# Gelu of the state-space output beside its split, and residual-gate pieces spread over the first attention's fill

## The chip, the cores and the metric

The kernel runs on one core of one Trainium2 chip, as one program of 17,119 instructions. The metric is the device time of one execution in microseconds (us); a run of the kernel is given by its median over several executions. The engines are TensorE (PE; its weight loads PEld), VectorE (DVE), ScalarE (ACT), GpSimd (POOL) and SyncE (SP), whose queue here issues most of the loads.

## The reference

Two transformer blocks follow each other on 512 tokens of width 1024, in float32. The change lies in the first block. Cut to what matters there:

```
mod = silu(c) @ w_ada + b_ada;  shift, scale, gate = split(mod, 3)
h = rms_norm(x, norm_g) * (1 + scale) + shift
ssm_u, ssm_z, q, k, v, attn_z, q_idx, k_idx, w_idx = split(h @ w_in)
y = complex diagonal state-space scan of ssm_u, by groups of 16 channels
z = gelu(y);  z = z * sigmoid(z @ w_glu + b_glu)
y_ssm  = z * silu(ssm_z)
y_attn = sparse_attention(q, k, v, index scores) * silu(attn_z)
x = x + gate * (concat([y_ssm, y_attn]) @ w_out)
```

So the gelu has one reader, the gated product with `w_glu` and the factor in front of it; and the third of `w_ada` that gives `gate` (the residual gate) is read only where the block's output is added to `x`.

## The kernel before

All large products are made of three float32r products: a weight or an activation is split into a rounded half ("hi", one copy on ACT, L145) and the rest ("lo", one subtraction on DVE, L146), and `mm3` (L153 to L155) multiplies hi by hi, lo by hi and hi by lo. `wchunk` loads a weight piece of 512 KB into a tile `wraw` (three buffers), splits it into `whi` and `wlo` (four buffers each), and the products run over it. Activations lie transposed; `hT` is the normalised input in its two halves.

The first block runs in stages. After the projections, index scores and the scan, the attention over eight heads runs as the main stream (`attend`), about 11 us a head. Each head needs transposes of its keys (L734) and, every second head, of its queries (L727); ACT and DVE take their halves out of PSUM (`ksth`, `kstl`, `qst`). Scores are products on PE (L341, L342) into one of two PSUM tiles `ps_s`; DVE adds the mask tile `bm` and takes the row minimum (L343), ACT makes the exponential (L345), DVE the reciprocal (L752), POOL and DVE the scaling (L350, L352); PE transposes the result (L369) into one of two PSUM tiles `ps_t`, ACT copies it out (L375), and PE multiplies by the values (L383). The mask tiles have one buffer each and POOL makes them (L744, L745), so those of the next head wait for L343 of this one.

Beside it runs the fill: `weave` draws as many products of the remaining projections as the main stream allows. Before the change the fill is, in order: what is left of the attention's gate columns (`ga`, two weight pieces), all eight pieces of the residual gate (`gate_sums`), the first half of the state-space gate columns (`gs`, two pieces), the split of the gelu's output `z` into `zT` (`z_split`), the second half of `gs` (two pieces), and the product with `w_glu` (two pieces). A piece of the residual gate is a load of 512 KB into a `wraw` buffer on SP (L897) and one multiply-and-sum of 128x1024 on DVE (L898); it has no product on PE. The gelu itself is the last step of `ssm_out` (L1330, four tiles of 128x512, `zg` from `zi`), which ends before the attention begins.

PE and SP execute in the order in which the program is written. ACT, DVE and POOL are ordered by a list scheduler at build time; on the chip each engine then executes its list strictly in order, so an instruction that waits holds up all behind it.

Of the kernel before, what the change touches and what calls it, by code (L numbers as in the profile page):

```python
# [11 lines left out]
AF = mybir.ActivationFunctionType  # L12
# [92 lines left out]
class Kern:  # L105
# [139 lines left out]
    def both(self, *streams):  # L245
        for g in streams:
            yield from g

    def hold(self, time):
        yield time  # L250
# [197 lines left out]
    def block1(self):  # L448
        nc, A, tc = self.nc, self.A, self.tc
# [14 lines left out]
        hT = [self.pages("hT" + x, 8, F32R) for x in "hl"]  # L464
# [126 lines left out]
        w_in = A["w_in"]  # L591
# [60 lines left out]
        def proj(n, dst):  # L652
            s8 = sm.tile([128, 4, 8], F32, name="s8", tag="s8", bufs=2)

            def ev(j, c, p):
                if c == 0:
                    dst.append(self.pg("qk"))
                nc.scalar.copy(dst[j][:, c:c + 256], p)
                sq = sm.tile([128, 256], F32, name="sq5", tag="q256", bufs=2)
                nc.scalar.activation(sq, p, AF.Square)  # L660
                nc.vector.tensor_reduce(s8[:, j, c // 64:c // 64 + 4], sq.rearrange("p (h d) -> p h d", d=64), axis=AX.X, op=OP.add)

            yield from self.gemm_tn(hT, 8, w_in, n, 512, ev)
            sums.append(s8)
# [11 lines left out]
        def ev_gs(j, p):  # L676

            gates[0].append(self.pg("gs"))
            nc.scalar.activation(gates[0][j], p, AF.Tanh, scale=0.5)
            STT(out=gates[0][j], in0=gates[0][j], scalar=1.0, in1=p, op0=OP.add, op1=OP.mult)  # L680

        def ev_ga(j, p):
# [4 lines left out]
        z = self.pages("zg", 4)  # L687
        fill = self.both(proj(1024, qf), proj(1536, kf), self.gemm_tn(hT, 8, w_in, 2048, 512, ev_v),
                         self.gemm_nt(hT, 8, self.cols(w_in, 2560, 512), ev_ga))
# [96 lines left out]
        zT = []  # L786

        def z_split():
            zT.extend(self.pages("zT" + x, 4, F32R) for x in "hl")
            for k in range(4):  # L790
                self.split(z[k], zT[0][k], zT[1][k])
                yield 0.0

        fill = self.both(fill, self.gate_sums(), self.gemm_nt(hT, 8, self.cols(w_in, 512, 256), ev_gs), z_split(),
                         self.gemm_nt(hT, 8, self.cols(w_in, 768, 256), lambda j, p: ev_gs(2 + j, p)),
                         self.gemm_nt(zT, 4, self.cols(A["w_glu"], 0, 512), ev_glu))
        self.weave(self.attend([head(h) for h in range(8)], more=1.4), fill)
        self.dump("y", y[0])
        attp.__exit__(None, None, None)
# [502 lines left out]
    def ssm_out(self, z):  # L1302


        nc = self.nc
        zi = self.pages("zi", 4)
        zd = self.dr.tile([4, 128, S], F32, name="zdram")
        for q in range(2):
            p = [self.ps((128, 512), "t") for _ in range(2)]
            for m in range(8):  # L1310
                a = q * 8 + m
                o = [v[:, m * 64:(m + 1) * 64] for v in p]
                for b in range(2):
                    nc.tensor.matmul(o[b], lhsT=self.TO[:, :, :, 2 * a + b], rhs=self.U(2 * a + b), start=True, stop=False)  # L1314
                for x in range(2):
                    for b in range(2):
                        s = slice(b * 64, b * 64 + 64)
                        nc.tensor.matmul(o[b], lhsT=self.F[x][a // 4][s, a % 4 * 128:(a % 4 + 1) * 128], rhs=self.St[x][s, a, 0:64],  # L1318
                                         start=False, stop=x == 1)
                yield 1.3  # L1320
            for b in range(2):
                O = self.pg("O")
                nc.scalar.copy(O, p[b])
                nc.scalar.dma_start(zd[2 * q + b], O)
        yield 2.0
        for n in range(4):
            nc.sync.dma_start(zi[n].rearrange("p (t k) -> p t k", t=8), zd[n].rearrange("(t c) (g k) -> (c g) t k", t=8, g=8))
        yield 0.0
        for n in range(4):
            nc.scalar.activation(z[n].rearrange("p (k t) -> p t k", t=8), zi[n].rearrange("p (t k) -> p t k", t=8), AF.Gelu_apprx_tanh)  # L1330
        self.dump("z", z)


    def block2(self):
# [525 lines left out]
```

## Time and profile before

| | us |
|---|---|
| median of 3 runs (1253.65 to 1254.65) | 1253.88 |
| the profiled execution | 1255.27 |
| its span, first to last instruction | 1253.5 |
| PE, DVE, ACT, POOL busy in it | 1159.3, 815.6, 552.8, 459.5 |
| attention of the first block, about | 254 to 372 |

The sum of a change is made against the profiled execution, whose own time is 1.39 us above the median. The chain that ended last runs for 76% of the span through PE and for 15% through DVE. In the timelines a row gives the start, the duration, the engine, the line, the tiles, the shape, and in brackets how long the engine had been idle before it and what released it. A busy PE can still be slow: the granted clock is given by stretch.

### The profile page before, as it was taken

To read this page: it belongs to the slowest core of one execution; us is meant where nothing else is said; L and a number is where in the kernel's file an instruction comes from. 1 tells how busy PE (TensorE), PEld (TensorE's weight loads), DVE (VectorE), ACT (ScalarE), POOL (GpSimd) and SP (SyncE) were. 2 spreads that over 40 slices of the span, in tenths; PEclk is the share of its full clock that TensorE was granted. 3 is DMA by queue.
4 is the path that set the end of the run, shared out by engine and by line. 5 is a ranking of instruction groups with operands and counts; after the bars stand their busy time and mean duration, and the time that the engine had idled before them with its cause. 6 is when DMAs were issued, how large, how long until landed. Compare 5 with 4: busy or idle time off the path is not lost.

```text
span 1253.5 us, 17119 instructions
## 1 busy us (share of the span) xinstructions
PE 1159.3 (92%) x6264; PEld 949.0 (76%) x6264; DVE 815.6 (65%) x1587; ACT 552.8 (44%) x1038; POOL 459.5 (37%) x546
## 2 busy tenths in 40 slices
PE   2786888977899999989999999999999999999998
PEld 2576887955678998977777777788888888888876
DVE  6887999267755466795667666554677743677731
ACT  4434432065744444555565656333544421344420
POOL 3869998068522135355656565201000000000000
PEclk9897989988999999998999999999999999999999
DMA  9452122163134532221111111134333223333330
GB/s 356 143 154 67 35 85 72 35 210 110 34 121 154 154 107 87 85 75 51 38 47 35 34 35 34 52 119 132 101 101 100 83 91 97 106 96 86 103 106 34
DMA packets 112755, 118.05 MB, mean 94 GB/s; under 512 B 16184, under 2 KB 101216, under 8 KB 112672
## 3 DMA queue, kind: packets, MB, share of 16 engines
q1 hardware_dynamic: 102432, 107.20, 27.1%
q10 hardware_dynamic: 10240, 9.77, 2.4%
q8 instruction: 49, 0.80, 0.3%
q14 instruction: 34, 0.28, 0.1%
HBM read 109.47 MB, written 6.30 MB: 92 GB/s over the span
## 4 chain that ended last, share of the span: by engine, by line
PE 76%; DVE 15%; ACT 3%; POOL 2%; issue 2%; DMA 1%; SPq 0%; ACTq 0%; DVEq 0%; POOLq 0%
PE ps_g L153 20%; PE ps_g L154 20%; PE ps_g L155 19%; PE ps_t L369 4%; PE ps_o L383 4%; DVE wlo L146 2%; PE ps_s L342 2%; PE ps_s L341 2%; DVE wada L490 1%; PE ps_t L1314 1%; DVE score L965 1%; DVE score L948 1%; PE ps_o L1652 1%; DVE t L1059 1%; PE ps_t L1318 1%
## 5 line engine op out<-in xcount | busy, mean ns | idle before, releaser
L145 ACT CAST whi<-wraw 128x1024 fp32r<-128x1024 f32 (+4 forms) x161 | 161.6, 1010 | 170.2 <-PE ps_g L154 146.7
L146 DVE TENSOR_TENSOR wlo<-wraw,whi 128x1024 fp32r<-128x1024 f32 (+4 forms) x143 | 175.8, 1235 | 61.3 <-ACT whi L145 60.8
L153 PE MATMUL ps_g<-hT,whi 128*128 128x512 f32 x504 | 205.1, 407 | 0.0
L155 PE MATMUL ps_g<-hT,wlo 128*128 128x512 f32 x504 | 198.9, 395 | 0.0
L154 PE MATMUL ps_g<-hT,whi 128*128 128x512 f32 x504 | 198.1, 393 | 0.0
L350 POOL TENSOR_TENSOR P<-P,rsum 128x256 f32<-128x256 f32 (+3 forms) x144 | 100.6, 728 | 77.9 <-DVE rsum L1439 29.7
L345 ACT ACTIVATE P<-P,nm 128x128 f32<-128x128 f32 (+3 forms) x160 | 89.6, 560 | 84.0 <-DVE nm L343 82.8
L153 PEld LDWEIGHTS ps_g<-hT,whi 128*128 128x128 f32 x504 | 95.2, 189 | 26.0 <-issue 9.3
L155 PEld LDWEIGHTS ps_g<-hT,wlo 128*128 128x128 f32 x504 | 95.0, 189 | 19.9
L154 PEld LDWEIGHTS ps_g<-hT,whi 128*128 128x128 f32 x504 | 95.3, 189 | 18.8 <-issue 1.2
L343 DVE CUSTOM_DVE_ANT_0 P<-ps_s,att 128x128 f32<-128x128 f32 (+3 forms) x128 | 62.1, 485 | 51.4 <-PE ps_t L369 26.9
L369 PE MATMUL ps_t<-consts,P 128*128 128x128 f32 x400 | 67.5, 284 | 12.2 <-DVE qst L889 7.1
L153 PE MATMUL ps_g<-whi,hTh 128*128 128x256 f32 x192 | 60.7, 316 | 13.8 <-DVE iq L886 8.0
L153 PE MATMUL ps_g<-act,whi 128*128 128x512 f32 (+1 forms) x176 | 70.2, 399 | 0.0
L154 PE MATMUL ps_g<-act,whi 128*128 128x512 f32 (+1 forms) x176 | 69.1, 393 | 0.0
L155 PE MATMUL ps_g<-act,wlo 128*128 128x512 f32 (+1 forms) x176 | 69.0, 392 | 0.0
L369 PEld LDWEIGHTS ps_t<-consts,P 128*128 128x128 f32 x400 | 47.6, 143 | 27.3 <-issue 14.9
L849 POOL TENSOR_TENSOR acc<-acc,sq 128x512 f32<-128x512 f32 x15 | 21.9, 1462 | 118.0 <-ACT sq L848 115.5
L154 PE MATMUL ps_g<-wlo,hT 128*128 128x256 f32 (+1 forms) x208 | 58.7, 282 | 2.4 <-DVE wlo L146 2.4
L153 PE MATMUL ps_g<-whi,hT 128*128 128x256 f32 (+1 forms) x208 | 59.0, 284 | 1.4 <-ACT sq L1354 1.4
L154 PE MATMUL ps_g<-wlo,hTh 128*128 128x256 f32 x192 | 56.3, 293 | 4.0 <-DVE wlo L146 4.0
L155 PE MATMUL ps_g<-whi,hT 128*128 128x256 f32 (+1 forms) x208 | 58.6, 282 | 0.0
(509 smaller groups left out, 2916.1 us busy)
## 6 DMA issues: line engine op xcount, KB each, us to landing
wraw<-in_w_in_dram SPq DMA_DIRECT2D x56, 512.0 KB, 3.6
wraw<-in_w_up_dram SPq DMA_DIRECT2D x40, 512.0 KB, 3.6
wada<-in_w_ada_dram SPq DMA_DIRECT2D x16, 512.0 KB, 7.4
wraw<-in_w_down_dram SPq DMA_DIRECT2D x16, 512.0 KB, 3.4
wadag<-in_w_ada_dram SPq DMA_DIRECT2D x8, 512.0 KB, 4.5
wraw<-in_w_out_dram SPq DMA_DIRECT2D x8, 512.0 KB, 3.4
wraw<-in_w_attn_br_dram SPq DMA_DIRECT2D x8, 512.0 KB, 3.4
wraw<-in_w_o_dram SPq DMA_DIRECT2D x8, 512.0 KB, 3.5
```

The lines of the kernel that those rows point to most:

```text
L145: nc.scalar.copy(hi, src)
L146: (eng or nc.vector).tensor_tensor(out=lo, in0=src, in1=hi, op=OP.subtract)
L153: mm(out, lhsT=l[0], rhs=r[0], start=start, stop=False)
L154: mm(out, lhsT=l[0], rhs=r[1], start=False, stop=False)
L155: mm(out, lhsT=l[1], rhs=r[0], start=False, stop=stop)
L341: nc.tensor.matmul(s, lhsT=q, rhs=khi[:, :w], start=True, stop=False)
L342: nc.tensor.matmul(s, lhsT=q, rhs=klo[:, :w], start=False, stop=True)
L343: nc.vector.tensor_tensor_reduce(out=P[i], in0=s, in1=madd(i), scale=-1.0, scalar=3.0e38, op0=OP.add, op1=OP.min, accum_out=nm[:, i:i + 1])
L345: nc.scalar.activation(P[i], P[i], AF.Exp, scale=-1.0, bias=nm[:, i:i + 1], accum_out=sums[:, i:i + 1])
L350: nc.gpsimd.tensor_tensor(out=P[n], in0=P[n], in1=sc[:, n:n + 1].to_broadcast([128, (n + 1) * 128]), op=OP.mult)
L369: nc.tensor.transpose(pt[:, o:o + 128], P[i][:, j * 128:(j + 1) * 128], self.ident)
L383: nc.tensor.matmul(acc[x * 64:(x + 1) * 64, j * 128:], lhsT=V(j), rhs=tiles[b][:, o:o + w], start=start and j == 0, stop=stop and j == 2)
```

## The change

The four gelu instructions leave the end of `ssm_out` and are issued in `z_split`, just ahead of the split of their output. `gate_sums` leaves its place in the fill's sequence; a new helper `between` runs the rest of the fill and issues one piece of the residual gate after every 4.0 us of estimated product time (a step of three 128x512 products counts as 0.648, so one piece after every seven steps). What is computed stays the same.

```diff
--- before.py
+++ after.py
@@ -245,6 +245,16 @@
     def both(self, *streams):
         for g in streams:
             yield from g
+
+    def between(self, main, other, every):
+
+        due = every
+        for got in main:
+            yield got
+            due -= got
+            if due <= 0 and next(other, None) is not None:
+                due = every
+        self.go(other)
 
     def hold(self, time):
         yield time
@@ -788,12 +798,14 @@
         def z_split():
             zT.extend(self.pages("zT" + x, 4, F32R) for x in "hl")
             for k in range(4):
+                nc.scalar.activation(z[k].rearrange("p (k t) -> p t k", t=8), self.zi[k].rearrange("p (t k) -> p t k", t=8), AF.Gelu_apprx_tanh)
+            for k in range(4):
                 self.split(z[k], zT[0][k], zT[1][k])
                 yield 0.0
 
-        fill = self.both(fill, self.gate_sums(), self.gemm_nt(hT, 8, self.cols(w_in, 512, 256), ev_gs), z_split(),
-                         self.gemm_nt(hT, 8, self.cols(w_in, 768, 256), lambda j, p: ev_gs(2 + j, p)),
-                         self.gemm_nt(zT, 4, self.cols(A["w_glu"], 0, 512), ev_glu))
+        fill = self.between(self.both(fill, self.gemm_nt(hT, 8, self.cols(w_in, 512, 256), ev_gs), z_split(),
+                                      self.gemm_nt(hT, 8, self.cols(w_in, 768, 256), lambda j, p: ev_gs(2 + j, p)),
+                                      self.gemm_nt(zT, 4, self.cols(A["w_glu"], 0, 512), ev_glu)), self.gate_sums(), 4.0)
         self.weave(self.attend([head(h) for h in range(8)], more=1.4), fill)
         self.dump("y", y[0])
         attp.__exit__(None, None, None)
@@ -1326,9 +1338,7 @@
         for n in range(4):
             nc.sync.dma_start(zi[n].rearrange("p (t k) -> p t k", t=8), zd[n].rearrange("(t c) (g k) -> (c g) t k", t=8, g=8))
         yield 0.0
-        for n in range(4):
-            nc.scalar.activation(z[n].rearrange("p (k t) -> p t k", t=8), zi[n].rearrange("p (t k) -> p t k", t=8), AF.Gelu_apprx_tanh)
-        self.dump("z", z)
+        self.zi = zi
 
 
     def block2(self):
```

On PE the order of the instructions does not change. On SP, from the last loads of the scan's output (`zi`) to the loads of `w_out`, there stood before:

```order
L1327 DMA zi<-zdram 128x8x64 x4
L174 DMA wraw<-in_w_in_dram 128x4x256 x2
L897 DMA wadag<-in_w_ada_dram 128x1024 x8
L174 DMA wraw<-in_w_in_dram 128x4x256 x4
L174 DMA wraw<-in_w_glu_dram 128x4x256 x2
L174 DMA wraw<-in_w_out_dram 128x4x256 x4
```

and now:

```order
L1339 DMA zi<-zdram 128x8x64 x4
L174 DMA wraw<-in_w_in_dram 128x4x256 x2
L909 DMA wadag<-in_w_ada_dram 128x1024 x3
L174 DMA wraw<-in_w_in_dram 128x4x256 x2
L909 DMA wadag<-in_w_ada_dram 128x1024 x2
L174 DMA wraw<-in_w_in_dram 128x4x256 x2
L909 DMA wadag<-in_w_ada_dram 128x1024 x2
L174 DMA wraw<-in_w_glu_dram 128x4x256
L909 DMA wadag<-in_w_ada_dram 128x1024
L174 DMA wraw<-in_w_glu_dram 128x4x256
L174 DMA wraw<-in_w_out_dram 128x4x256 x4
```

`wadag` are the pieces of the residual gate, `wraw` the weight pieces; they share three buffers. The loads of the `gs` weights now stand behind three pieces and not behind eight, and the last piece stands between the two loads of `w_glu`. In the program as it is built the sixth, seventh and eighth pieces lie in the same buffer of the three; before, the eight went round all three.

On ACT around the first keys and queries of the attention there stood before:

```order
L148 ACTIVATE ksth<-ps_t,gq 128x512
L888 ACTIVATE qst<-ps_t,gq 64x512
L1330 ACT_TABLE_LOAD
L1330 ACTIVATE zg<-zi 128x8x64
L888 ACTIVATE qst<-ps_t,gq 64x512
L1330 ACTIVATE zg<-zi 128x8x64 x2
L148 ACTIVATE ksth<-ps_t,gq 128x512
L1330 ACTIVATE zg<-zi 128x8x64
L684 ACTIVATE ga<-ps_g 128x512
L145 CAST whi<-wraw 128x1024 x2
L345 ACT_TABLE_LOAD
L345 ACTIVATE P_2594,sums<-P_2594,nm 128x128
```

These rows are the gelu with a load of its function table, and then the load of the exponential's table. Now the gelu stands in the middle of the sixth head's exponentials, in a row, with a table load on either side:

```order
L385 COPY pt_3133<-ps_t 128x512
L145 CAST whi<-wraw 128x1024
L689 ACTIVATE gs<-ps_g 128x512
L801 ACT_TABLE_LOAD
L801 ACTIVATE zg<-zi 128x8x64 x4
L355 ACT_TABLE_LOAD
L355 ACTIVATE P_3118,sums<-P_3118,nm 128x256
L145 CAST zTh<-zg 128x512
L385 COPY pt_3217<-ps_t 128x256
L148 ACTIVATE ksth<-ps_t,gq 128x512
L355 ACTIVATE P_3119,sums<-P_3119,nm 128x384
L145 CAST zTh<-zg 128x512
```

What moved is the gelu, past about 50 instructions of ACT. `P` are the exponentials, `pt` the copies of transposed tiles out of PSUM.

On DVE the last two pieces of the residual gate (L910 here, with the gate's sum, L915) stand in the third head's work now:

```order
L910 ISA gate 128x1
L362 TENSOR_SCALAR P_2685<-P_2685,rsum 128x384
L362 TENSOR_SCALAR P_2686<-P_2686,rsum 128x512
L353 ISA P_2770,nm<-ps_s,bm_2619 128x256
L353 ISA nm 128x1
L146 TENSOR_TENSOR wlo<-wraw,whi 128x1024
L695 SCALAR_TENSOR_TENSOR ga<-ga,ps_g 128x512
L910 ISA wadag,gate<-wadag,cB 128x1024
L910 ISA gate 128x1
L901 SCALAR_TENSOR_TENSOR qst<-ps_t,gq,qst 64x512
L915 TENSOR_TENSOR gate<-gate,vecs 128x8
```

L353 is the line that was L343 before. Before, the eighth piece stood ahead of the second head's third tile; the two `qst` rows had no piece ahead of them.

## Rows read from the trace of the kernel before

**Rows 1.** Page, part 1: busy us (share of the span) and instructions of each engine

```profile
PE 1159.3 (92%) x6264; PEld 949.0 (76%) x6264; DVE 815.6 (65%) x1587; ACT 552.8 (44%) x1038; POOL 459.5 (37%) x546
```

**Rows 2.** Busy times by stretch: length; busy of each engine; granted clock; DMA

```profile
260.00:265.00 5.00, 0.78 (x2) 0.50 (x2) 2.24 (x3) 4.97 (x7) 1.22 (x4) 0.59 0.22 86
...
320.00:330.00 10.00, 9.03 (x41) 6.88 (x42) 6.73 (x16) 7.43 (x19) 5.68 (x8) 0.83 0.13 46
```

**Rows 3.** Timeline of ACT, 255 to 266 us: start, duration, line, tiles, [idle before]

```profile
255.12 0.67 ACT L888 ACTIVATE qst<-ps_t,gq 64x512 fp32r<-64x512 f32 x1
255.81 1.28 ACT L1330 ACT_TABLE_LOAD   x1
257.10 1.17 ACT L1330 ACTIVATE zg<-zi 128x512 f32<-128x512 f32 x1
...
261.70 1.12 ACT L1330 ACTIVATE zg<-zi 128x512 f32<-128x512 f32 x1
...
263.14 1.98 ACT L145 CAST whi<-wraw 128x1024 fp32r<-128x1024 f32 x2
265.13 1.28 ACT L345 ACT_TABLE_LOAD   x1
```

**Rows 4.** Timeline of PE, 257 to 299 us

```profile
257.53 1.20 PE L734 MATMUL ps_t<-consts,kn 128*128 128x128 f32 x4
...
264.22 0.79 PE L153 MATMUL ps_g<-hTh,whi 128*128 128x512 f32 x1 [4.78 <-ACT whi L145]
...
298.91 0.66 PE L369 MATMUL ps_t<-consts,P 128*128 128x128 f32 x2 [3.73 <-DVE qst L889]
```

**Rows 5.** Timeline of DVE, 264 to 299 us

```profile
264.20 2.36 DVE L146 TENSOR_TENSOR wlo<-wraw,whi 128x1024 fp32r<-128x1024 f32 x2 [0.24 <-ACT whi L145]
...
270.11 1.23 DVE L898 CUSTOM_DVE_ANT_0 wadag<-wadag,cB 128x1024 f32<-128x1024 f32 x1 [2.40 <-DMA wadag<-in_w_ada_dram]
...
271.26 0.28 DVE L343 CUSTOM_DVE_ANT_0 P<-ps_s,bm 128x128 f32<-128x128 f32 x1
...
294.64 1.25 DVE L146 TENSOR_TENSOR wlo<-wraw,whi 128x1024 fp32r<-128x1024 f32 x1
...
298.01 0.75 DVE L889 SCALAR_TENSOR_TENSOR qst<-ps_t,gq,qst 64x512 fp32r<-64x512 f32 x1 [0.75 <-ACT qst L888]
```

**Rows 6.** Timeline of POOL: first mask tile of the second head

```profile
271.63 1.54 POOL L745 TENSOR_TENSOR bm<-consts,BT 128x128 f32<-128x128 f32 x1 [10.42 <-DVE nm L343]
```

**Rows 7.** DMA issues at 255.0, 265.4, 267.7, 277.5, 279.9: count, size, us to landing

```profile
wraw<-in_w_in_dram SPq DMA_DIRECT2D x2, 512.0 KB, 6.8
...
wadag<-in_w_ada_dram SPq DMA_DIRECT2D x1, 512.0 KB, 4.5
...
wadag<-in_w_ada_dram SPq DMA_DIRECT2D x1, 512.0 KB, 5.1
...
wadag<-in_w_ada_dram SPq DMA_DIRECT2D x1, 512.0 KB, 3.2
...
wraw<-in_w_in_dram SPq DMA_DIRECT2D x1, 512.0 KB, 3.6
```

**Rows 8.** Tile of residual-gate rows: DVE's products, ns min/median/max

```profile
L898 DVE CUSTOM_DVE_ANT_0 wadag<-wadag,cB x8: 1208/1226/1811, 266.5 to 283.5; 128x1024 f32<-128x1024 f32 x8
```

**Rows 9.** Timeline of ACT, 327 to 335 us

```profile
327.43 0.60 ACT L679 ACTIVATE gs<-ps_g 128x512 f32<-128x512 f32 x1
...
331.25 0.37 ACT L375 COPY pt<-ps_t 128x256 f32<-128x256 f32 x1 [0.66 <-PE ps_t L369]
...
334.44 0.59 ACT L375 COPY pt<-ps_t 128x512 f32<-128x512 f32 x1 [0.94 <-PE ps_t L369]
```

**Rows 10.** Timeline of PE, 333 to 340 us: transposes and a score product

```profile
333.69 0.66 PE L369 MATMUL ps_t<-consts,P 128*128 128x128 f32 x4
...
335.05 0.63 PE L369 MATMUL ps_t<-consts,P 128*128 128x128 f32 x4
...
339.10 0.39 PE L341 MATMUL ps_s<-ksth,qst 128*128 128x512 f32 x1
```

## The prediction

> **What bounds the kernel now.** The page's first part comes first: PE is busy 92% of the span [rows 1], so whatever moves no wait of PE moves nothing, and the question is where PE stands still between 254 and 372 us, the stage of the change. The table of stretches shows two weak ones there. From 260 to 265 PE is busy 0.78 of 5 us while ACT is busy 4.97; from 320 to 330 PE is at 9.03 of 10 with a granted clock of 0.83, which is 1.7 us of full-speed work lost [rows 2]. Then the timelines, engine by engine. On ACT the reader is to see the stretch before 265 us: a table load of 1.28, four gelus of 1.12 to 1.17 with a `qst` and a `ksth` between them, and only behind them, at 263.14, the two casts `whi` [rows 3]. On PE these casts end a wait of 4.78 at 264.22; the other long wait, 3.73, ends at 298.91 with the second `qst` half of DVE [rows 4]. On DVE the second gate piece waits 2.40 for its load at 270.11, and the first score tile, at 271.26, stands behind it [rows 5]. POOL's first mask tile of the second head waits 10.42 for that tile [rows 6]. So the start of this stage is a ladder: gelu, casts, subtraction, second piece's load, first score tile, masks of the next head.
>
> **First part: the gelu leaves the front.** It removes from ACT one table load (1.28) and four gelus between 255.81 and 262.82 [rows 3]; the second table load, at 265.13, lay in idle time of ACT. What is late next? The second head's keys are transposed by 257.53 + 1.20 = 258.73 [rows 4]; a `ksth` and a `ga` of about 0.65 each follow, so ACT could begin `whi` at 260.1, 3.0 earlier. The raw weights bound it too: the second of the two loads issued at 255.0 lands 6.8 later, 261.8 [rows 7], the first somewhat sooner; if both came together the gain is only 1.3. I take 260.5, near ACT's own bound, because the casts go one after the other and only the second needs the later load: 2.6 us earlier. PE restarts at 261.6 instead of 264.22.
>
> The subtraction `wlo` [rows 5] moves by the same 2.6, and so do the reuse of its buffer by the second piece, that piece's load of 4.5 us [rows 7], its product, and the first score tile: 271.26 becomes 268.7. The first two pieces still stand ahead of that tile on DVE, so the wait for the second piece's load isn't removed, only moved.
>
> **Second part: the pieces are spread.** No piece goes away: eight loads and eight products of 1.23 (up to 1.81 where POOL works beside them) [rows 8] still run. SP is passed by nothing but these loads; the weight loads of the next columns come sooner than they are needed. What is new is that pieces six, seven and eight use one buffer, so each load can be issued only after the product before it has run, and DVE, which executes in order, stands at each product until the load lands. Behind the waiting product stand score tiles, scalings, and for the eighth the two `qst` whose end releases PE at 298.91. Loads alone take 3.2 to 3.6, with others in flight 4.5 to 5.1 [rows 7]. The ladder on DVE, from 268.7:
> the first tile (0.28) and piece three end at 270.2; the load of piece four, with weight loads in flight, 4.3, and its product: 275.8; a subtraction (1.25), a score tile (0.28), a `kstl` (0.75, as `qst`) and a reciprocal (0.2): 278.3; piece five: 279.5; piece six, load 3.6 and product 1.25: 284.4; piece seven the same: 289.2; piece eight the same: 294.1; the first `qst` 0.75, ACT's copy for the second 0.67, the second 0.75: 296.3. The other work of DVE, ACT and POOL in this time fits into the waits. Before, that `qst` ended at 298.01 + 0.75 = 298.76 [rows 5]. So the front gives **2.5 us earlier**, which is about what it gave at the start: the spread neither adds nor takes much, but it stands on four load times. At 3.2 each the ladder is 2.3 shorter (4.8 earlier); at 4.5 for the three that share a buffer it is 2.7 longer (0.2 later). I take 3.6, the nearest row to a single load beside little else. From there to 327 PE runs as before and carries the shift.
>
> **Third part: the gelu arrives in the sixth head.** In times of before, ACT ends `gs` at 328.0 [rows 9]. Now 1.28 + four gelus in a row (4 x 1.14, less 0.1 overlap each) + 1.28 follow: 6.9 us [rows 3] in which ACT does nothing else. Queued behind are an exponential (0.5), a `zTh` cast (0.55) and the copy `pt` that frees a PSUM tile. That copy began at 331.25 after an idle time of 0.66; now it begins at 336.0 and ends at 336.3. PE's transposes of 333.69 [rows 10] need the tile: 2.7 late. The next ones, of 335.05, need the key tile that `kstl` frees: about 338.0, 2.9 late. The score product of 339.10 [rows 10] needs a tile that DVE frees, and DVE now has the last two `zTl` ahead of it, which wait for ACT's last two `zTh`, at about 340.4: two `zTl`, one `yp`, one score tile later it is 343.0, 3.9 late. After that ACT's lag is no larger than PE's, the product with `w_glu` needs `zT` only at 350, and nothing more is added. ACT's idle time, such as the 0.66 and 0.94 [rows 9], is what hides the rest of the 6.9. I take **3.9 later**, with 2.7 (only the first wait counts) and 6.9 (nothing hidden) as bounds.
>
> The row for table loads is 1.28, and the gelu begins 0.01 after it, the load 0.02 after the `qst` before it [rows 3]: no drain shows. The Trainium skill (page "ScalarE: Activation LUTs", section "What ACT_TABLE_LOAD costs") counts a drain of 1.38 us with every switch, 2.66 together; the trace disagrees. By the page the block would be 2.8 longer, as a rival below.
>
> **Sum.** -2.5 + 3.9 = +1.4. On the profiled execution, 1255.27, that is 1256.7; it stood 1.39 above the median, so for the median 1253.88 + 1.4 = **1255.3 us**.
>
> **Rivals.**
> - The front gives more than the block takes. For it: the loads that share a buffer run alone, so 3.2 [rows 7] is possible and the front becomes 4.8, with ACT's own bound of 3.0 at its start 5.2; if PE's wait before the second `qst` goes as well, half of the 1.7 that a fall of the clock costs [rows 2] is saved, 0.8. With the block at its lower bound of 2.7 this is -3.3: 1250.6. Against it: the first eight-piece burst is gone, but the weight loads now lie between the pieces. Chance 0.22.
> - It ends slower: pieces on a single buffer become DVE's bound. For it: the trace already has one such wait of 2.40 [rows 5], and three in a chain have no lookahead. It decides once a load takes over 4.4, the front then giving nothing (+0.2); with the block at 3.9 and a clock that falls after PE's waits there as it does at 320 to 330 (1.7 [rows 2]), that is +5.8: 1259.7. Against it: between these pieces DVE has work of its own that covers part of each wait. Chance 0.24.
> - Table loads that stall ACT longer in the middle of dense work than in the sparse front: two times 1.38 more in the block, hidden by nothing, +4.2: 1258.1. It is the page's rule as a mechanism here; the rows are against it. Chance 0.04.
>
> **How the numbers follow.** About 0.2% (2.5 us) is what a measurement of this kernel can tell from no change, so "same" is 1251.4 to 1256.4. The forecast has 0.50, with its own range 1252.9 to 1257.6 (front 1.3 to 4 earlier, block 3 to 5 later); of it 0.38 lies within the bound, 0.10 slower, 0.02 faster. With the rivals: faster 0.22 + 0.02 = 0.24, same 0.38, slower 0.10 + 0.24 + 0.04 = 0.38. The range takes in the first rival and the second nearly whole: 1250.2 to 1259.5.
>
> **What the profile after would show.** Right: on PE the wait before the first `w_in` product shrinks from 4.78 to about 2; on DVE the pieces six to eight each wait for their load, and the second `qst` half that releases PE ends near 296; on ACT a block of about 7 us at 326 with two table loads of 1.28; PE waits of about 2.7 and 0.9 behind it. Wrong: pieces that never wait (then the first rival), a `qst` that ends at 299 or later (the second), a gap of over a microsecond beside the table loads (the third), or PE running through the gelu block without a wait, by which the change would be faster than I say.

## The result, and the profile after

The changed kernel is slower: 1263.31 us median (4 runs, 1259.78 to 1264.72) against 1254.27 of the kernel before (1253.65 to 1254.69); ratio 1.0060, 95% interval 1.0045 to 1.0075. Two later comparisons gave 1.0058 (1.0044 to 1.0073) and 1.0056 (1.0040 to 1.0073). The ratios are those on record for the runs of both kernels, not quotients of the medians, which lie 9.0 apart here; by the ratios the change costs 7.0 to 7.5 us, where +1.4 was predicted. Either way the result lies outside the predicted range. The profiled execution took 1264.63, its span is 1262.6, 9.1 longer than before. PE's work is the same but for a slower clock (busy time as in [rows 1], by engine):

```profile
PE 1163.8 (92%) x6264; PEld 952.1 (75%) x6264; DVE 815.9 (65%) x1587; ACT 552.7 (44%) x1038; POOL 460.2 (36%) x546
```

The table of stretches (length; busy PE, PEld, DVE, ACT, POOL; granted clock; DMA share and GB/s), where [rows 2] answer to the first two:

```profile
260.00:265.00 5.00, 3.25 (x10) 1.77 (x10) 3.60 (x5) 3.27 (x4) 3.19 (x9) 0.80 0.64 223
320.00:330.00 10.00, 8.20 (x34) 6.77 (x34) 4.88 (x15) 6.14 (x13) 4.09 (x8) 0.66 0.17 52
330.00:345.00 15.00, 12.52 (x61) 8.62 (x60) 8.88 (x19) 13.65 (x25) 6.35 (x9) 0.89 0.12 37
```

[Rows 2] overstate the difference: this execution lies 2.0 us behind that profile when it reaches 250 us, ahead of every edit. A second profile of the kernel before (experiment 5) lies only 0.3 from this one there, and its stretches are the fair ones to compare:

```profile
260.00:265.00 5.00, 1.69 (x8) 0.83 (x6) 1.51 (x2) 4.92 (x7) 3.54 (x10) 0.82 0.71 249
320.00:330.00 10.00, 6.78 (x32) 5.76 (x32) 5.94 (x14) 6.22 (x14) 4.03 (x7) 0.83 0.16 52
330.00:345.00 15.00, 15.00 (x86) 11.25 (x85) 12.81 (x31) 10.94 (x28) 9.92 (x15) 1.00 0.12 37
```

The front is better, PE works 3.25 us of the first stretch in place of 1.69. In the third stretch PE stood still nowhere before; now ACT is busy 13.65 of 15 us and PE stands still for 2.5. PE's timeline, in the order in which it happens ([rows 4, 10] answer):

```profile
263.03 0.79 PE L153 MATMUL ps_g<-hTh,whi 128*128 128x512 f32 x1 [1.62 <-ACT whi L145]
...
279.75 0.78 PE L744 MATMUL ps_t<-consts,kn 128*128 128x128 f32 x4 [4.67 <-DVE rsum L762]
...
288.83 0.66 PE L379 MATMUL ps_t<-consts,P 128*128 128x128 f32 x4 [1.76 <-ACT pt L385]
...
298.62 0.66 PE L379 MATMUL ps_t<-consts,P 128*128 128x128 f32 x2 [5.60 <-DVE qst L901]
...
338.27 1.12 PE L393 MATMUL ps_o<-pt,V 128*64 128x256 f32 x2 [2.48 <-ACT pt L385]
339.32 1.12 PE L379 MATMUL ps_t<-consts,P 128*128 128x128 f32 x4
...
345.75 0.40 PE L351 MATMUL ps_s<-ksth,qst 128*128 128x512 f32 x1
```

The wait for `whi` fell from 4.78 to 1.62. The wait at 298.62, for the second `qst` half, is longer than its partner in [rows 4], 5.60 for 3.73. As the two profiles stand it ends 0.29 earlier, and 2.3 earlier once the 2.0 from ahead of the edit are taken off. At 338.27 stands a wait that before didn't have: a product with the values waits for ACT's copy `pt`. The score product of 339.10 [rows 10] is at 345.75. Who holds that copy up is read on ACT, and who holds `qst` up on DVE ([rows 9] and [rows 5] answer; in the last rows ACT's copy for the first `qst` half stands with DVE's):

```profile
329.44 0.60 ACT L689 ACTIVATE gs<-ps_g 128x512 f32<-128x512 f32 x1
330.06 1.28 ACT L801 ACT_TABLE_LOAD   x1
331.35 4.18 ACT L801 ACTIVATE zg<-zi 128x512 f32<-128x512 f32 x4
335.55 1.28 ACT L355 ACT_TABLE_LOAD   x1
336.84 0.51 ACT L355 ACTIVATE P<-P,nm 128x256 f32<-128x256 f32 x1
...
337.86 0.36 ACT L385 COPY pt<-ps_t 128x256 f32<-128x256 f32 x1
```

```profile
269.13 1.22 DVE L910 CUSTOM_DVE_ANT_0 wadag<-wadag,cB 128x1024 f32<-128x1024 f32 x1 [2.57 <-DMA wadag<-in_w_ada_dram]
...
276.17 1.23 DVE L910 CUSTOM_DVE_ANT_0 wadag<-wadag,cB 128x1024 f32<-128x1024 f32 x1 [0.55 <-DMA wadag<-in_w_ada_dram]
...
285.32 1.52 DVE L910 CUSTOM_DVE_ANT_0 wadag<-wadag,cB 128x1024 f32<-128x1024 f32 x1 [0.68 <-DMA wadag<-in_w_ada_dram]
...
290.15 1.32 DVE L910 CUSTOM_DVE_ANT_0 wadag<-wadag,cB 128x1024 f32<-128x1024 f32 x1 [0.36 <-DMA wadag<-in_w_ada_dram]
...
293.64 0.67 ACT L900 ACTIVATE qst<-ps_t,gq 64x512 fp32r<-64x512 f32 x1
...
294.97 1.21 DVE L910 CUSTOM_DVE_ANT_0 wadag<-wadag,cB 128x1024 f32<-128x1024 f32 x1
...
296.22 0.74 DVE L901 SCALAR_TENSOR_TENSOR qst<-ps_t,gq,qst 64x512 fp32r<-64x512 f32 x1
...
297.72 0.75 DVE L901 SCALAR_TENSOR_TENSOR qst<-ps_t,gq,qst 64x512 fp32r<-64x512 f32 x1 [0.55 <-ACT qst L900]
```

The gelu block is 6.7 us of ACT without a gap over 0.02. The pieces that share a buffer hardly wait (0.68, 0.36, nothing), and DVE is busy 22.8 of the 26 us from 272 to 298. ACT has its copy for the first `qst` half ready at 294.31, but on DVE the eighth piece stands ahead of that half, which starts at 296.22; the second ends at 298.47. Before, no piece stood there.

**Against which profile.** The first profile of the kernel before is an early one. A second profile of it (experiment 5) runs 2.3 us behind the first at 250 us and gains 1.9 of them back later, 1.2 of it at 570 us, so that both spans agree (1253.5 and 1253.8). Below, a kernel's lead (negative) or lag (positive) is its PE row's start less that of the same product in this second profile, in us; what a stage changes is the difference of two columns, and the column of 250 us is what an execution brings along from ahead of the edit:

| profile | 250 | 301 | 327 | 337 | 482 | 505 | 606 |
|---|---|---|---|---|---|---|---|
| changed, first | -0.3 | -2.5 | -0.2 | +4.4 | +4.4 | +5.9 | +8.8 |
| changed, third (experiment 15) | -0.9 | -1.5 | -1.5 | +3.1 | +3.0 | +4.9 | +5.4 |
| gelu alone moved (1) | -0.6 | -4.0 | -4.0 | +0.5 | +1.1 | +1.1 | +2.7 |
| pieces alone spread (2) | 0.0 | +0.5 | +2.3 | +1.6 | +2.2 | +3.8 | +5.4 |
| gelu behind the casts (6) | +0.1 | -1.5 | -0.1 | -0.1 | -0.2 | -0.2 | -0.1 |

Two steps are steady: +4.3 to 5.3 between 327 and 337 in all five profiles with the gelu in the sixth head, and +1.5 to 1.9 between 482 and 505 wherever the pieces are spread by 4.0 and the order of experiment 9 isn't put back. Others come in one execution and not in the next: the changed kernel lost 2.3 between 301 and 327 in its first profile, nothing in its third. Further on, 1.5 to 1.7 are lost at 527 us in nine of the 18 profiles, bursts (1 and 3) among them, and 1.0 to 1.3 at 570 in seven; the changed kernel's first profile has both, its third neither. They are left out of the account of the change.

### The profile page after: what moved, and what is told of

It is laid out like the page before. It is cut to its first block, busy times and chain, and to the rows that moved or that the text cites. A ratio compares the mean times of both kernels' runs of the same rounds, so it can differ in the third digit from the quotient of the medians.

```text
span 1262.6 us, 17114 instructions
## 1 busy us (share of the span) xinstructions
PE 1163.8 (92%) x6264; PEld 952.1 (75%) x6264; DVE 815.9 (65%) x1587; ACT 552.7 (44%) x1038; POOL 460.2 (36%) x546
## 4 chain that ended last, share of the span: by engine, by line
PE 77%; DVE 15%; ACT 3%; DMA 2%; issue 2%; POOL 1%; ACTq 0%; SPq 0%; DVEq 0%; POOLq 0%
PE ps_g L153 20%; PE ps_g L155 20%; PE ps_g L154 20%; PE ps_t L379 4%; PE ps_o L393 4%; DVE wlo L146 2%; PE ps_s L352 2%; PE ps_s L351 2%; DVE wada L500 1%; DMA wadag<-in_w_ada_dram 1%; PE ps_t L1326 1%; PE ps_o L1662 1%; DVE score L977 1%; DVE t L1071 1%; DVE score L960 1%
## 5 line engine op out<-in xcount | busy, mean ns | idle before, releaser
L353 DVE CUSTOM_DVE_ANT_0 P<-ps_s,att 128x128 f32<-128x128 f32 (+3 forms) x128 | 62.1, 485 | 51.7 <-PE ps_t L379 27.1
```

What stands on the lines that cost most here:

```text
L353: nc.vector.tensor_tensor_reduce(out=P[i], in0=s, in1=madd(i), scale=-1.0, scalar=3.0e38, op0=OP.add, op1=OP.min, accum_out=nm[:, i:i + 1])
```

## The experiments

Times are medians, ratios with 95% intervals against the kernel before, timed beside it on the same chip (1 to 4, 5 to 8, 9 to 12 and 13 to 16 share a chip each). A ratio difference of 0.001 is about 1.25 us; where two ratios are subtracted, the uncertainty given behind the difference combines their two intervals.

**The two parts, one at a time.** Experiment 1 takes the changed kernel and puts the pieces back into a burst:

```diff
-        fill = self.between(self.both(fill, self.gemm_nt(hT, 8, self.cols(w_in, 512, 256), ev_gs), z_split(),
+        fill = self.both(fill, self.gate_sums(), self.gemm_nt(hT, 8, self.cols(w_in, 512, 256), ev_gs), z_split(),
...
```

> Only the gelu moves to the sixth head; the eight pieces of the residual gate stay in one burst in the fill. Theory (the gelu block in the sixth head is what costs, 4.6 us in the changed kernel's profile, and the gain of the front, 2.3, belongs to the gelu that left it): about +2.5 to +4.5 us on the kernel before, with the value product's wait on pt of about 2.5 at 338 us again. Rival one (the spread pieces are what costs): about -2 to 0. Rival two (what lies outside the stage, 2.0 before it and 3.2 behind it, belongs to the new program and not to either part): over +6.

Measured: 1258.41, ratio 1.0019 (1.0011 to 1.0028), +2.4 us, a little under the theory's range, with the wait on `pt`, 2.53 at 334.45, of the size expected. Experiment 2 keeps the spread and puts the four gelus back to the end of `ssm_out`:

```diff
...
-        self.zi = zi
+        for n in range(4):
+            nc.scalar.activation(z[n].rearrange("p (k t) -> p t k", t=8), zi[n].rearrange("p (t k) -> p t k", t=8), AF.Gelu_apprx_tanh)
```

> Only the pieces of the residual gate are spread, one behind every 4 us of products; the gelu stays in front of the attention. Theory (the block costs, the spread does little): 0 to +1.5 us. Rival one (the spread costs: three pieces on one buffer hold up DVE and the clock falls behind PE's waits): +5 to +8, and the second qst half of DVE ends at 299.5 or later. Rival two (terms outside the stage): +4 to +5 with an undisturbed stage.

Measured: 1259.39, ratio 1.0033 (1.0019 to 1.0047), +4.1. The theory (0 to +1.5) is missed, and so is the first rival's range. The number lies in the second rival's (+4 to +5, terms outside the stage), but not its picture: 1.6 are lost at 505 us, outside the stage, and 1.6 by 330 us, inside it. The spread costs more than the block less its front gain, but not the whole loss. Both parts lose, and 2.4 + 4.1 is 6.5 of the 7.3 that experiment 4, the changed kernel on the same chip, shows:

> The changed kernel once more, on the chip of the three others. Theory: +7 to +9 us as measured, its executions between 1259 and 1265. Rival (part of the 9 us was one chip or one hour): under +5. If the terms outside the stage (2.0 before 254 us, 3.2 behind 500) are chance, the profile shows other ones there than in the first profile, with the stage's own -2.3, +2.3 and +4.6 again.

Measured: 1263.83, ratio 1.0058. The loss holds, and the profile has the stage's steps again: 2.0 earlier at 301 (0.5 of it from ahead of the stage), 1.9 lost to 327, 4.3 to 337.

**What the gelu costs where.** Experiment 3 issues it behind the second gate-column piece's split:

```diff
+        def gelu_behind(stream):
+            done = False
+            for got in stream:
+                if not done and len(gates[1]) >= 2:
+                    done = True
+                    for k in range(4):
+                        nc.scalar.activation(z[k].rearrange("p (k t) -> p t k", t=8), self.zi[k].rearrange("p (t k) -> p t k", t=8), AF.Gelu_apprx_tanh)
+                yield got
```

> The gelu leaves ACT's front but is issued right behind the split of the second gate-column weight piece, where ACT stood idle from 265 to 271 us; the residual gate's pieces stay in one burst. Theory (front gain is real, block is the cost): the front's 2.3 to 3 stays and no block follows, so -2 to -3 us, 1251 to 1252. Rival one (the front's gain needs the spread, since the burst of pieces sets the second qst): about 0. Rival two (a new program loses 5 outside the stage): +2 to +4.

Measured: 1257.73, ratio 1.0014 (1.0006 to 1.0023). The theory's -2 to -3 was missed, because the list scheduler put the gelu ahead of the casts, not behind them; ACT's timeline:

```profile
262.22 1.28 ACT L810 ACT_TABLE_LOAD   x1
263.52 3.87 ACT L810 ACTIVATE zg<-zi 128x512 f32<-128x512 f32 x4
267.18 2.00 ACT L145 CAST whi<-wraw 128x1024 fp32r<-128x1024 f32 x2
```

PE then waits 6.72 for `whi`. So this run doesn't test what it was made for; it tells that the casts are what counts in the front. Experiment 6 ties the gelu to the second cast:

```diff
...
-                    for k in range(4):
+                    with self.tc.issue_after(self.hi.ins):
+                        for k in range(4):
...
```

> The gelu is issued behind the second cast of the second gate-column weight piece, so that it and its two table loads (6.4 us) fall into ACT's idle time of 6.3 us before the first exponential; the residual gate's pieces stay in one burst. Theory (the front gains what the gelu leaves in front of the casts, 3.5 us at PE's first product behind them, and the block in the sixth head is gone): 3 to 4 us earlier than before at 299 us, nothing lost between 299 and 345, and 2 to 5 us less than the kernel with the gelu alone in the sixth head; against before -1 to -3. Rival (the first exponential is late by the block and the queue of ACT behind it takes the gain back): within 0.5 of before at 299 us.

Measured: 1254.15, ratio 0.9977 (0.9967 to 0.9987), -2.9: the first kernel that beats before. In experiment 1 ACT stood idle for 6.31 between these casts and the first exponential; the block of 6.8 fills that and delays the exponential by 0.7:

```profile
262.35 2.20 ACT L145 CAST whi<-wraw 128x1024 fp32r<-128x1024 f32 x2
264.57 1.28 ACT L811 ACT_TABLE_LOAD   x1
265.86 4.20 ACT L811 ACTIVATE zg<-zi 128x512 f32<-128x512 f32 x4
270.08 1.28 ACT L355 ACT_TABLE_LOAD   x1
271.37 0.41 ACT L355 ACTIVATE P<-P,nm 128x128 f32<-128x128 f32 x1
```

In its profile the lead of 3.3 us at 267 us was down to 1.5 at 301 and gone at 327, where 3 to 4 at 299 and nothing lost behind it were expected. PE's waits from 272 us on are those of experiment 1 within 0.1, so most of this is the clock (granted 0.86 from 300 to 312 us, 1.00 in experiment 1); the profiled execution is one of its longer ones (1255.51, of 1251.38 to 1255.81). The gelu leaving the front is worth 2.9 in time (0.0023, give or take 0.0010). Experiments 1 and 6 differ by where the gelu goes alone: 0.0042, so the block in the sixth head costs **5.3 us**, give or take 1.6, more than in the gap behind the casts.

Experiment 7 leaves the gelu out of the changed kernel, experiment 8 puts a tanh in its place, for which the trace shows no table load:

```diff
...
-            for k in range(4):
-                nc.scalar.activation(z[k] ..., self.zi[k] ..., AF.Gelu_apprx_tanh)
+            z[:] = self.zi          (experiment 7)
+                nc.scalar.activation(z[k] ..., self.zi[k] ..., AF.Tanh)          (experiment 8)
...
```

> The changed kernel without its gelu: the split and the product with w_glu take the gelu's input as it is (the output is another), the pieces stay spread. Theory (block 4.6 us, the rest is the spread's): 4 to 5 us below the changed kernel, the loss of about 2 between 299 and 326 us still there, and no wait of the value product on pt. Rival (most of the block's loss is the clock behind PE's waits that the spread makes, not ACT): 2 or less below.

> The changed kernel with a tanh in the gelu's place (the gelu is left out): the same four instructions, no table load on either side. Theory (PE is late by what ACT is late, less a slack of about 2.3, so that every us off the block counts in full): the block is 4.3 in place of 6.7 on ACT and PE loses about 2 in place of 4.6: 2 to 3 us below the changed kernel. By the Trainium skill's count of a drain with each switch it would be over 5. Rival (the four gelus alone fill ACT enough to hold PE up): under 1.

Measured: 1258.67, ratio 1.0016 (1.0002 to 1.0029), and 1258.42, ratio 1.0016 (1.0004 to 1.0028). Both stand 0.0042 below the changed kernel of experiment 4 (on another chip, each against its own before), again 5.3 us, give or take 2.5. Leaving the block out gives back what the theory said (4 to 5) or a little more. The tanh gives back more than the theory's 2 to 3: without the two table loads, 2.56 us of ACT, as much is saved as without the whole block, within this uncertainty. Its ACT timeline shows why:

```profile
329.49 4.24 ACT L801 ACTIVATE zg<-zi 128x512 f32<-128x512 f32 x4
333.47 0.47 ACT L355 ACTIVATE P<-P,nm 128x256 f32<-128x256 f32 x1
...
334.44 0.37 ACT L385 COPY pt<-ps_t 128x256 f32<-128x256 f32 x1
```

These 4.2 us are nearly hidden: PE has no wait on this copy, loses 0.2 between 327 and 337, and 0.5 more by 372, 0.7 in place of the changed kernel's 4.6. What exceeds them, 2.56, is close to the wait of 2.48 in the changed kernel, and behind the wait the matmuls run at half the clock (the transposes of 339.32 last 1.12, those in [rows 10] 0.66). No other wait lies in this stretch, so the clock is what is left of the 4.6, about 2. The changed kernel's stretches there:

```profile
336.00:339.00 3.00, 0.73 (x2) 0.29 (x2) 0.85 (x2) 2.99 (x7) 0.23 (x1) 0.85 0.00 0
339.00:342.00 3.00, 3.00 (x13) 2.39 (x13) 2.42 (x5) 3.00 (x8) 1.02 (x2) 0.58 0.03 5
```

The Trainium skill (page "ScalarE: Activation LUTs", section "What ACT_TABLE_LOAD costs") counts a drain of 1.38 with each switch. The saving of 5.3 happens to be the page's 2 x 2.66, but the rows tell otherwise: the load at 330.06 begins 0.02 behind the activation before it, and from the end of `gs` to the exponential ACT takes 6.80 in the changed kernel and 3.87 with the tanh, 2.9 less, not 5.3.

**What before itself does.** Experiment 5 takes the kernel before once more:

> The kernel before, once more, with a second profile. All five profiles of changed kernels lose 1.7 to 2.4 us between 189 and 199 us, ahead of every edit, against the first profile of the kernel before. Theory (those 2 us belong to the one profiled execution of before, by chance of how the bias tables' loads and the clock fell): the second profile stands 1.5 to 2.5 us behind the first at 250 us, and its time is no different from before's median. Rival (they belong to the changed programs): the second profile runs as the first at 250 us, within 0.3.

Measured: 1256.38, ratio 1.0002 (0.9991 to 1.0013); the theory holds. The second profile has the 2 us before 250, at a transpose of the bias tables in the index scores' stage, where the first profile waits 4.03 and this one 5.97:

```profile
200.54 2.07 PE L930 MATMUL ps_t<-btf,consts 128*128 128x512 f32 x2 [5.97 <-ACT BT L931]
...
266.52 0.80 PE L153 MATMUL ps_g<-hTh,whi 128*128 128x512 f32 x1 [4.77 <-ACT whi L145]
```

**What the spread costs.** In the second block, 170 us behind the edit, the order of ACT's list had changed. The kernel before (second profile), then the changed kernel's ACT and PE there:

```profile
501.20 0.47 ACT L1397 ACTIVATE qr<-ps_g,rs 128x256 f32<-128x256 f32 x1 [0.93 <-PE ps_g L155]
501.57 0.47 ACT L1354 ACTIVATE sq<-ps_g,rs 128x256 f32<-128x256 f32 x1
```

```profile
505.56 0.84 ACT L1407 ACTIVATE qr<-ps_g,rs 128x256 f32<-128x256 f32 x2 [1.67 <-PE ps_g L155]
506.29 0.84 ACT L1364 ACTIVATE sq<-ps_g,rs 128x256 f32<-128x256 f32 x2
```

```profile
506.81 0.39 PE L153 MATMUL ps_g<-whi,hT 128*128 128x256 f32 x1 [1.29 <-ACT sq L1364]
```

Two copies now run ahead of two squares; the first square frees a PSUM tile, and PE waits 1.29 for it. Neither profile of the kernel before waits at this product; a wait for an earlier square, 1.4 to 1.5 some 7 us ahead, is in all of them. Experiment 9 is experiment 2 with the pair order put back, and nothing else:

```diff
...
-                nc.scalar.activation(qr[j][g][:, c:c + 256], p, AF.Copy, scale=rt(j))
+                with self.tc.issue_after(self.sq_ins):
+                    nc.scalar.activation(qr[j][g][:, c:c + 256], p, AF.Copy, scale=rt(j))
```

> The kernel with the spread alone, with one order put back: in the second block's query projection ACT again makes each square behind its own copy (copy, square, copy, square), where the spread had made it copy, copy, square, square and PE waited 1.29 for a square at 504 us. Theory (1.3 to 1.5 of the spread's cost arise there, 170 us behind the edit): 1.3 to 1.5 us below the kernel with the spread alone, so +2.5 on before in place of +4. Rival (another wait takes its place or the clock gives it back): under 0.5 below.

Measured: 1258.49, ratio 1.0035 (1.0022 to 1.0047), 5 executions. The wait was gone from the profile, but the ratio is no lower than that of experiment 2 (1.0033), which is what the rival said; across two chips and with 5 executions this decides little. Experiments 13 to 16 ran both pairs on one chip:

> The spread alone, once more, as the partner of the next one on the same chip. Both theories: +3.5 to +4.5 on before.

> The spread alone with the order of the squares in the second block put back. Theory (that order is a term of 1.4): 1 to 2 below its partner. Rival (what is gained there is lost again behind it to the clock, as the fall of 1.6 at 526 us that the first profile of this kernel shows and that of its partner doesn't): within 0.5 of its partner.

> The changed kernel, as the partner of the next one. Both theories: +7 to +8 on before.

> The changed kernel with the order of the squares put back. Its fall of the clock at 526 us is there without this edit, so that nothing new is to be lost behind it. Theory: 1 to 2 below its partner. Rival: within 0.5 of it.

Measured: 1261.30, ratio 1.0039 (1.0024 to 1.0054), against 1259.00, ratio 1.0019 (1.0008 to 1.0029); and 1263.61, ratio 1.0056, against 1260.97, ratio 1.0037 (1.0024 to 1.0051). Time follows the order in both pairs, by 0.0020 and 0.0019, some **2.4 us**, give or take 1.8 for the two pairs together, a little over the theory's 1 to 2. The profiles show 1.5 to 1.9 at the spot; whether there is more is open, since the interval is wide enough for there to be none, and 2 against 9 showed no difference at all. In experiment 16, with the order put back, ACT reads so, and PE doesn't wait:

```profile
505.46 0.47 ACT L1408 ACTIVATE qr<-ps_g,rs 128x256 f32<-128x256 f32 x1 [0.93 <-PE ps_g L155]
505.83 0.47 ACT L1364 ACTIVATE sq<-ps_g,rs 128x256 f32<-128x256 f32 x1
```

What is left of the spread, 2.4 (0.0019 in experiment 14, with 0.0008 to 0.0029; the same kernel had 0.0035 in experiment 9), arises in the first heads: at 330 us the profiles of 2, 9, 13 and 14 lie 0.5 to 3.3 later than at 250 us. Before, PE's waits between 272 and 299 us are many and shorter; the second profile of before has 2.65, 1.29, 1.54, 1.22 and 3.74, together 10.4. In the changed kernel's first profile they are 4.67, 1.76 and 5.60, together 12.0; in the other ten with pieces spread by 4.0, 10.0 to 12.7. The last wait is the steady one: 4.7 to 6.0 in these eleven, where the eighth piece (1.2 us of DVE) stands ahead of the first `qst` half, and 3.7 to 3.8 in the other seven, where none does. So the piece on DVE's way to `qst` is shown; that the rest of the 2.4 is the clock behind these longer waits is argued, not tested. POOL is a rival in this stretch, busy all of the 26 us from 272 to 298 in the first profiles of both kernels; DVE waits only 0.5 for it in the changed kernel, but no experiment takes work off POOL.

**Do the parts add up, and is there a better interval?** Experiment 10 has the gelu behind the casts, the spread, and the order put back; 11 has the gelu behind the casts and an interval of 8.0 (the order in the second block is then as before by itself); 12 has all eight pieces at the end of the fill, with the order put back.

```diff
...
-        self.gemm_nt(zT, 4, self.cols(A["w_glu"], 0, 512), ev_glu)), self.gate_sums(), 4.0)
+        self.gemm_nt(zT, 4, self.cols(A["w_glu"], 0, 512), ev_glu)), self.gate_sums(), 8.0)          (experiment 11)
+        self.gemm_nt(zT, 4, self.cols(A["w_glu"], 0, 512), ev_glu), self.gate_sums())          (experiment 12)
...
```

> The gelu behind the casts as in the kernel that beat before (-2.9), the pieces spread one for every 4 us (+4.1 alone), and the order of the squares in the second block put back (-1.4). If the parts add up, as gelu front -2.9, block +5.4 and spread +4.1 to the changed kernel's +7.3: -0.2 on before, and 7 below the changed kernel. Rival (the spread's cost in the front comes only from its meeting with the gelu in front of it): -2.9, as without the spread.

> The gelu behind the casts, and one piece of the residual gate for every 8 us of products in place of 4, so that half of the pieces leave the stretch from 265 to 300 us, where DVE is busy 25 of 28 us and PE waits 12. Theory (what holds PE up there is DVE's work, ten us of it the pieces; an interval of 4 only rearranges it): PE's waits there fall by 2 to 4 us, 3 to 6 below before. Rival (later pieces only meet another full stretch, the heads after 330): within 1 of the kernel with the gelu behind the casts and the pieces in a burst, -2.9 on before.

> The gelu behind the casts, the eight pieces at the end of the fill, behind the loads for the product with w_glu, and the order of the squares put back. Theory (as for an interval of 8, all eight pieces gone from the first heads, into 345 to 390 us where DVE is busy 0.55 of the time): 4 to 8 us below before. Rival (the loads of the next stage, w_out, now stand behind eight pieces in the same three buffers, and PE waits for them behind 372 us): no better than -2.9, with a new wait of PE for a weight cast between 360 and 385.

Measured: 1255.19, ratio 1.0005 (0.9997 to 1.0014), +0.6 us where -0.2 was expected, inside the interval (-0.4 to +1.8): the parts add up. Then 1252.01, ratio 0.9979 (0.9970 to 0.9988), and 1252.20, ratio 0.9983 (0.9972 to 0.9994): in both the rival's time held, no better than the burst with the gelu behind the casts, but not its place: experiment 12 has no new wait between 360 and 385 us (0.36 for `y`, as in experiment 6), and experiment 11 loses its lead ahead of 330 us, not behind. The theory was right on the waits of the front (PE's timeline of experiment 11, in the stretch of the 10.4):

```profile
277.59 0.66 PE L744 MATMUL ps_t<-consts,kn 128*128 128x128 f32 x4 [1.82 <-DVE kstl L149]
...
285.69 0.66 PE L379 MATMUL ps_t<-consts,P 128*128 128x128 f32 x4 [0.80 <-ACT pt L385]
...
293.59 0.41 PE L379 MATMUL ps_t<-consts,P 128*128 128x128 f32 x2 [3.71 <-DVE qst L909]
```

6.3 us of waits, and a lead of 7.5 over the second profile of before at 301 us (1.5 of it from ahead of the stage). But by 327 it is down to 4.6, through new waits (0.82, 0.56, 0.49, and 4.05 for the `qst` at 317.44) and the clock behind them. Experiments 6, 11 and 12 can't be told apart by their ratios; all three beat both kernels.

## Why the prediction was wrong

The mechanism of the gelu was right at both ends; the step that failed is the second part, and the sum misses a term outside the stage.

- **First part, the gelu leaves the front: right.** Predicted 2.6 earlier at the casts; PE's first product behind them comes 3.2 earlier, each profile counted from its own place at 250 us, in all eleven profiles in which the gelu is out of the casts' way, and 2.9 remain in time (experiment 6). `whi` began at 261.94, where 260.5 was taken; with the 2.0 from ahead of the edit taken off that is 259.9, near the 260.1 that the prediction called ACT's own bound.
- **Second part, "the spread neither adds nor takes much", with "from there to 327 PE runs as before and carries the shift": the step that failed.** The front term was -2.5; measured in time it is -2.9 for the gelu and +2.4 for the spread in the first heads, -0.5 together. The ladder itself ended nearly where it was put: with the 2.0 taken off, `qst` ended at 296.5, where 296.3 was predicted. That was partly luck. Its rungs were to be waits for loads, which were there in time (waits of 0.68, 0.36 and nothing); DVE's own work filled the ladder instead, and the second and third profile of the changed kernel have `qst` at 297.1 and 298.0 by the same count. What the ladder was set against was wrong: without the spread the lead is 3.5 at this point (experiment 1), so that the spread takes 1.2 to 2.8 of it there, with the eighth piece ahead of `qst`. Nor was the shift carried: at 330 us the three profiles stand 0.1 and 0.2 behind and 0.7 ahead of their place at 250 us, and experiment 1 still 3.5 ahead. The rival "pieces on a single buffer become DVE's bound" named the right engine with the wrong reason, and the signs misled: pieces that hardly wait were to mean the first, faster rival. (The prediction also laid the piece of 1.81 to POOL working beside it; POOL's row of 271.63 [rows 6] has a piece beside it too, at 271.64, and that took 1.23.)
- **The term that was missing**: some 2.4 us of the spread arise at 505 us. I compared the orders only in the stage of the change; the swapped pair of copies and squares stood in ACT's list and could have been read there.
- **Third part, the block: right mechanism, too small.** 3.9 predicted, 4.6 in the first profile, 5.3 in time. I put PE's wait at the transposes of 333.69; it was one product earlier, on the values, and I did not count what the clock takes behind a wait (about 2 of the 4.6). The wait on DVE that was to make it 3.9 did not come. The block's length was written as 6.9; its own terms give 6.7, and 6.7 was measured. The bound of nothing hidden was far off: 4.2 are hidden.
- **The table loads**: no drain in the rows, as predicted; without the two loads 5.3 us are saved by the ratios and 3.9 in the profile, because the block then ends within what PE can wait for.

The sum in ratios: -2.9 (front) + 5.3 (block) + 2.4 (spread, first heads) + 2.4 (order in the second block) is +7.2; measured +7.0 to 7.5. Each term is uncertain by 1 to 2 us, so that the close agreement is partly chance. Not settled is what decides whether the clock falls behind a given wait: between 301 and 327 us 2.3 us were lost in the first profile of the changed kernel and nothing in the third.

## What to carry to other kernels

Give a block of work on a shared engine a place by its length: where four activations of 4.2 us were nearly hidden, the block of 6.7 cost 5.3, and the same block in an idle gap of 6.3 left the kernel 2.9 faster than before. Where a scheduler orders the engines, compare the order of the whole program before and after, since an edit can swap instructions stages away. And a stretch in which one engine is busy nearly throughout (DVE here, 22.8 of 26 us) wasn't improved by spreading its work inside that stretch: a piece of 1.2 us then stood just ahead of what PE waited for.

## What the runs showed of the hardware

The granted clock falls behind PE's long waits, and for how long differs between executions of one program. The changed kernel's first profile, behind the wait of 5.60, and its third, behind one of 5.41:

```profile
297.00:300.00 3.00, 1.38 (x5) 1.22 (x6) 1.49 (x4) 1.24 (x3) 1.34 (x5) 0.52 0.61 191
300.00:303.00 3.00, 3.00 (x10) 2.31 (x9) 1.36 (x3) 1.92 (x5) 1.61 (x4) 0.50 0.00 1
303.00:306.00 3.00, 3.00 (x19) 2.65 (x18) 1.51 (x5) 1.55 (x6) 2.32 (x4) 0.84 0.02 5
```

```profile
297.00:300.00 3.00, 0.39 (x3) 0.42 (x3) 1.85 (x5) 0.68 (x1) 0.79 (x2) 0.86 0.85 268
300.00:303.00 3.00, 3.00 (x10) 2.38 (x9) 1.01 (x3) 1.77 (x4) 1.08 (x2) 0.57 0.13 44
303.00:306.00 3.00, 3.00 (x23) 2.61 (x21) 2.35 (x8) 1.65 (x5) 2.67 (x5) 1.00 0.02 5
```

0.50 is the lower of the two levels, 1.2 of 2.4 GHz. One program's executions spread over up to 7 us here (the kernel before 1252.9 to 1259.9 on one chip); how much of this is the clock no run shows. A single profile's lead of 2 us at some place is no evidence by itself.
